# Who makes the lower parts of the expert weights: VectorE alone in place of VectorE and GpSimd

## The chip, the cores and the metric

The kernel runs on one core of a Trainium2 chip. The metric is the device time of one execution in microseconds (us). The kernel before took 1891.57 us, the median of three runs (1889.69 to 1892.58).

## What is computed

One layer of a decoder trunk on 1024 tokens of width 1024. The larger part of it (a modulated norm, one input projection, a recurrent branch, an attention over selected keys, a merge and an output projection) is not touched. The change lies in the mixture of experts that follows: each token goes to 2 of 32 experts, and each expert is a gated network.

```python
def expert_block(args):
    xb, e = args
    hid = jax.nn.silu(xb @ w1[e]) * (xb @ w3[e])   # w1, w3: 1024 x 512
    return hid @ w2[e]                              # w2: 512 x 1024
...
h = h + g2[:, None, :] * hier_moe(u2, ...)
return rmsnorm(h, final_g)
```

All is in float32.

## The kernel before

**Two parts of a number.** TensorE takes each float32 operand as a rounded upper part and a lower part, the rest. ScalarE (ACT) makes the upper part by a copy, and another engine makes the lower part as the difference of the raw number and the upper one. A product of two operands is then three products: upper with upper, upper with lower, lower with upper.

**An expert's weights.** `expert_weights` (L1356 and on) cuts an expert's three matrices into six chunks of 128 x 2048 numbers (1 MB): two of w1, two of w3, two of w2. SP issues each load (`raw_load`, L1377) into a tile of a ring. The ring has 13 tiles at first and shrinks to 7 on the way: `RU` tells how often each of the last places is used. A tile can be loaded again when both engines have read the chunk in it.

`weights` inside `expert` (L1463 to L1475) takes a chunk in two halves of 128 x 1024, g = 0 and 1. For each half it issues the copy `whi` on ACT (L1472) and the subtraction `wlo` (L1474). There are 6 tiles for `whi` and 4 for `wlo` that rotate. Which engine subtracts is decided in one line:

```python
eng = nc.gpsimd if name[0] != "2" and name[-1] == "0" and (g == 1 if e else name[0] == "1") else nc.vector
```

The name is that of the matrix ("1", "3" or "2"), the expert and the chunk. So for every expert but the first, GpSimd (POOL) makes the second half of the first chunk of w1 and of w3, two of the twelve lower parts; for the first expert it makes the two halves of w1's first chunk. VectorE (DVE) makes the rest.

**One expert on the engines.** The rows of an expert's tokens are gathered by POOL's queue (`xg`, L1453), transposed on PE (`ptx`, L1483) and split into `xh` on ACT (L97) and `xl` on DVE (L98). PE sums w1's products in `pa` and w3's in `pb` (L1501), six products of 512 columns for each half chunk, 48 in all. ACT makes `hid` from `pa` (L1506), DVE multiplies it with `pb` (L1507), PE transposes it (`pth`), and it is split into `hh` and `hl`. Then 24 products with w2's parts go to `py` (L137 to L139). DVE scales the sum into `ye` (L1539, two halves), and POOL's queue adds it to the rows in memory by a scatter (`h_spill`, L1543).

Experts overlap. The loop in `experts` steps through the generators of expert e and e - 1 in turn, so that PE does w1 and w3 of one expert, and then w2 of the one before. Within the scheduler's order each engine runs its queue in order: what waits on DVE holds up all that stands behind it there. After the nineteenth expert a branch (`overflow`) takes further blocks of tokens, if an expert has more than 128. `combine` adds the last two experts' parts and makes the final norm.

Of the kernel before, what the change touches and what calls it, by code (L numbers as in the profile page):

```python
# [81 lines left out]
class Trunk:  # L82
# [18 lines left out]
    def as_traced(self, engines):  # L101
        """Each of these engines runs what the block traces in the order in which it is traced."""
# [88 lines left out]
    # ------------------------------------------------------------------  # L191
# [10 lines left out]
    def mod_acc(self, acc, j0, n, ring, last=1):  # L202
        """acc[p, :] = b_mod (row 0) + sum over k of silu(c)[k, p] * w_mod[k, p, :], one k at a time."""
# [15 lines left out]
    def head(self):  # L219
        """Modulated, normalised rows, transposed, and the latent's products, in the order that HEAD gives."""  # L220
        nc, tc, io = self.nc, self.tc, self.io
        x, wm = io["x"][0], io["w_mod"][0][:, : 2 * D].rearrange("p (s c) -> p s c", s=2)
        with ExitStack() as st:
# [53 lines left out]
            def C():  # L277
                """silu(c) as columns"""
                pv = psum("pcol")
                nc.tensor.transpose(pv[:, :KT], cr, self.ident[:KT, :KT])  # L280
                th = hp.tile([P, KT], F32, name="th")
                nc.scalar.activation(th, pv[:, :KT], AF.Tanh, scale=0.5)
                nc.vector.scalar_tensor_tensor(th, th, 1.0, pv[:, :KT], op0=OP.add, op1=OP.mult)
                nc.vector.tensor_scalar(self.csil, th, 0.5, None, op0=OP.mult)

            def Q():
                """The table of square roots comes with this one."""
# [27 lines left out]
            def b(q):  # L315
                """Sums over the partitions; every product's columns are alike, the first of each is left standing."""
# [10 lines left out]
            def e(q):  # L327
                """shift1 and scale1 as columns"""
# [73 lines left out]
    def rsqrt(self, out, m, pool):  # L402
# [5 lines left out]
        # one Newton step: r * (1.5 - 0.5 * m * r * r)  # L408
# [5 lines left out]
    def lru_params(self, lam, hp):  # L414
# [6 lines left out]
        # y = min(|lam|, 80); v = exp(-y) = 2^-n * exp(-f)  # L421
# [15 lines left out]
        # 2^-n from its exponent bits  # L437
# [4 lines left out]
        # log1p(v) = 2 atanh(v / (2 + v))  # L442
# [8 lines left out]
        # softplus(-lam) = max(-lam, 0) + log1p(v)  # L451
# [5 lines left out]
    # ------------------------------------------------------------------  # L457
    def load_in(self, c, m):
        # while the vector engine is taken up by the search, another splits the weights
# [5 lines left out]
    def in_order(self):  # L465
        """Column tiles of w_in in the order of their use, after the latent's."""
# [6 lines left out]
    def next_in(self):  # L473
        """The next column tile; the one after it is already on its way."""
# [6 lines left out]
    def project(self, c0, c1, evac, t0=0):  # L481
        """psum[cols, tokens] of u @ w_in for columns c0..c1, tokens t0.., in column tiles of 128."""
# [15 lines left out]
    def index(self):  # L498
# [4 lines left out]
        with ExitStack() as st:  # L503
            ip = self.pool(st, "idx")
            pp = self.ixp
            # latent
# [24 lines left out]
            # indexer keys: [hi; hi] and [lo; 0]  # L531
# [59 lines left out]
    # ------------------------------------------------------------------  # L591
    def search(self, st):
        """Exact top-256 of each row of scores -> additive bias (s - q) on the selected keys."""
# [33 lines left out]
        # rows whose 256th largest is negative are searched with the sign turned  # L627
        nc.vector.tensor_scalar(t0, cnt, float(TOPK), None, op0=OP.is_ge)
        nc.vector.tensor_scalar(sg, t0, 2.0, -1.0, op0=OP.mult, op1=OP.add)
        for i, j in enumerate(J):  # L630
            n = (j + 1) * P
            # R = 256 where the sign stays, n - 255 where it is turned
# [6 lines left out]
        # On ACT, the count of y >= T is at least R where sum(sign(y - T)) > 2 R - 1 - n, but for T equal to the  # L639
        # R-th value itself, where either may come out: the search ends on it or on the float before it.  # L640
# [22 lines left out]
        # where R or more lie above, the next float is the one  # L663
# [29 lines left out]
    # ------------------------------------------------------------------  # L693
    def gates_q(self, spans):
        """Merge gates and queries, kept in DRAM until their turn."""
# [24 lines left out]
    # ------------------------------------------------------------------  # L720
    def rnn(self):
        nc, io = self.nc, self.io
        with ExitStack() as st:
# [34 lines left out]
            def block(b, xc, xh, xl, gh, gl):  # L758
# [9 lines left out]
                # t = tanh(-log_a / 2), w0 = exp(log_a)  # L768
# [4 lines left out]
                # w = 1 / (1 + t) = (1 + a) / 2, from a = exp(log_a) by one Newton step  # L773
# [3 lines left out]
                # ti = 2 w sqrt(t) * (i x): w1 = -w  # L777
                nc.vector.scalar_tensor_tensor(sq, sq, -2.0, w1, op0=OP.mult, op1=OP.mult)
                nc.vector.tensor_tensor(ti, ti, sq, op=OP.mult)
                # a = 1 - 2 t w  # L780
# [20 lines left out]
    # ------------------------------------------------------------------  # L801
    def attention(self):
# [3 lines left out]
        with ExitStack() as st:  # L806
# [8 lines left out]
            def prep(h):  # L815
                """Keys, queries and, for two heads at a time, values."""
# [131 lines left out]
    # ------------------------------------------------------------------  # L948
    def merge(self, keep, ph):
        """mixT = sigmoid(mgA) * y_aT + sigmoid(mgB) * y_bT."""  # L950
# [26 lines left out]
        # the last places of ring_a hold the merged branches first, 256 tokens in each  # L977
# [16 lines left out]
    def out_w(self, pool, ks):  # L994
        """w_out times gate1, a row block of 128 at a time."""
# [3 lines left out]
        # by halves of the columns, the first half where memory is needed soonest  # L999
# [10 lines left out]
    def branch_load(self, st, br, src, nk, side, g, places):  # L1010
        nc = self.nc
        gp = self.pool(st, f"yg{br}", side=side)
        # in the order of their places, so that the first to be loaded lie where memory is free first
# [10 lines left out]
    def branch_w(self, w, br, nk, c):  # L1024
        """Parts of a column tile, by row blocks; those beyond the eighth in tiles of their own."""
# [45 lines left out]
    def mod_rows(self, st):  # L1071
        """g1, shift2, norm2_g * (1 + scale2), g2 as rows on every partition."""
# [28 lines left out]
    def route_weights(self, st):  # L1101
        """[group | unused | expert] router columns times norm2_g * (1 + scale2), and shift2 through them plus
        the bias, on every partition."""
# [31 lines left out]
    # ------------------------------------------------------------------  # L1135
    def project_out(self):
        """h = x + g1 * (mix @ w_out); u2 rows to DRAM; the routing of each token."""
# [575 lines left out]
```

## Time and profile before

| | |
|---|---|
| median of the runs | 1891.57 us |
| profiled execution (its own time is told by the span alone) | 1894.4 us |
| PE busy | 1778.8 us, 94% |
| DVE busy | 1470.3 us, 78% |
| ACT busy | 1173.6 us, 62% |
| POOL busy | 458.5 us, 24% |
| mean granted clock of TensorE | 0.982 of 2.4 GHz |
| moved by DMA | 366.85 MB |

The profile has one execution's instructions on each engine with start and length, the loads' landings and the semaphores. A group of rows puts alike instructions together: line, engine, operation, output and inputs, shape, count, then the busy time with the mean, then the idle time of the engine just before them with what ended it. A row of stretches gives each engine's busy time (and instructions) in a stretch, the granted clock, the busy share of the 16 DMA engines and what they moved. A product's record is longer than the distance to the next one, since products are pipelined, and a DVE record reaches about 0.07 us into the next one; distances from start to start are what counts.

### The profile page before, as it was taken

Reading aid. Unit: us, or ns where it says so; the run is one execution under the profiler, and the core shown is the slowest. Engines: PE = TensorE matmul, PEld = TensorE weight load, DVE = VectorE, ACT = ScalarE, POOL = GpSimd, SP = SyncE. Lnnn points to the kernel's source line nnn. Section 1 sums busy time; section 2 is a strip of 40 time slices with the busy share of each in tenths; the row PEclk is TensorE's granted clock in tenths of the full one; section 3 lists DMA queues with packets and bytes.
Section 4 is the critical chain, followed back from the end, with each engine's and each line's share of the span. In section 5 each row is a group of like instructions: output and inputs, shape, how many; then the busy total and the mean of one; then the engine's idle time right before and its main releaser. Section 6 shows DMA issues by size and latency. Waiting matters only on the chain.

```text
span 1894.4 us, 24650 instructions
## 1 busy us (share of the span) xinstructions
PE 1778.8 (94%) x8532; PEld 1458.3 (77%) x8532; DVE 1470.3 (78%) x2331; ACT 1173.6 (62%) x1730; POOL 458.5 (24%) x311
## 2 busy tenths in 40 slices
PE   3999999998999999999999989979999999999995
PEld 2788887776777889999788868858778787778774
DVE  6689877696776758777433366479999999999988
ACT  6565677726667758888321023258777777777665
POOL 4101012210010001222000010045454545454444
PEclk9999999998999999999999999979999999999998
DMA  9213754322211222111748444569989999999984
GB/s 295 57 34 111 241 176 150 103 72 65 72 48 61 67 82 75 56 59 60 237 139 265 139 162 178 190 232 354 332 317 333 372 361 364 352 371 359 341 307 157
DMA packets 163738, 366.85 MB, mean 194 GB/s; under 512 B 17855, under 2 KB 107543, under 8 KB 139160
## 3 DMA queue, kind: packets, MB, share of 16 engines
q1 hardware_dynamic: 152112, 340.50, 50.6%
q0 software_dynamic: 10192, 19.99, 4.2%
q10 hardware_dynamic: 1304, 4.74, 0.6%
q8 instruction: 68, 1.11, 0.3%
q14 instruction: 62, 0.51, 0.1%
HBM read 326.90 MB, written 54.53 MB: 201 GB/s over the span
## 4 chain that ended last, share of the span: by engine, by line
PE 56%; DVE 22%; ACT 9%; issue 8%; DMA 3%; POOL 2%; SPq 0%; DVEq 0%; ACTq 0%; POOLq 0%
PE pb L1501 8%; PE pa L1501 6%; DVE wlo L1474 5%; PE py L138 5%; PE py L137 5%; PE py L139 5%; PE pj L139 3%; PE pj L137 3%; PE pj L138 3%; ACT junk_a L654 2%; DVE xc L745 2%; DVE xl L98 1%; PE pout L138 1%; PE pout L137 1%; PE pout L139 1%
## 5 line engine op out<-in xcount | busy, mean ns | idle before, releaser
L1474 DVE TENSOR_TENSOR wlo<-raw_w,whi 128x1024 fp32r<-128x1024 f32 x320 | 479.2, 1542 | 10.2 <-PE pa L1501 3.8
L1472 ACT ACTIVATE whi<-raw_w 128x1024 fp32r<-128x1024 f32 x384 | 398.2, 1059 | 103.5 <-PE pa L1501 29.2
L139 PE MATMUL pj<-uhi,wlo_in 128*128 128x512 f32 (+2 forms) x784 | 303.6, 388 | 5.6 <-POOL wlo_in L128 4.4
L137 PE MATMUL pj<-uhi,whi_in 128*128 128x512 f32 (+2 forms) x784 | 305.1, 389 | 1.2 <-ACT gq L706 1.2
L138 PE MATMUL pj<-ulo,whi_in 128*128 128x512 f32 (+2 forms) x784 | 302.9, 386 | 0.0
L1474 POOL TENSOR_TENSOR wlo<-raw_w,whi 128x1024 fp32r<-128x1024 f32 x64 | 180.9, 2829 | 89.1 <-ACT whi L1472 42.5
L139 PEld LDWEIGHTS pj<-uhi,wlo_in 128*128 128x128 f32 (+1 forms) x784 | 147.0, 187 | 37.5 <-POOL wlo_in L128 6.3
L137 PEld LDWEIGHTS pj<-uhi,whi_in 128*128 128x128 f32 (+1 forms) x784 | 147.3, 188 | 32.3 <-ACT gq L706 2.3
L138 PEld LDWEIGHTS pj<-ulo,whi_in 128*128 128x128 f32 (+1 forms) x784 | 147.1, 188 | 30.2 <-issue 1.0
L654 ACT ACTIVATE junk_a<-B,nt 128x768 bf16<-128x768 f32 (+2 forms) x93 | 96.8, 1041 | 48.9 <-DVE nt L650 40.6
L128 POOL TENSOR_TENSOR wlo_in<-raw_in,whi_in 128x1024 fp32r<-128x1024 f32 (+1 forms) x20 | 51.0, 2550 | 232.8 <-ACT whi_in L127 232.8
L1501 PE MATMUL pa<-whi,xh 128*128 128x512 f32 x256 | 104.5, 408 | 0.6 <-ACT xh L97 0.5
L138 PE MATMUL py<-wlo,hh 128*128 128x512 f32 x256 | 100.8, 394 | 1.3 <-DVE wlo L1474 1.3
L1501 PE MATMUL pa<-whi,xl 128*128 128x512 f32 x256 | 101.6, 397 | 0.1
L137 PE MATMUL py<-gh,whi_y 128*128 128x512 f32 x256 | 99.8, 395 | 1.5 <-ACT gh L97 1.5
L139 PE MATMUL py<-gh,wlo_y 128*128 128x512 f32 x256 | 100.4, 393 | 0.0
L138 PE MATMUL py<-gl,whi_y 128*128 128x512 f32 x256 | 100.3, 394 | 0.1
L1501 PE MATMUL pb<-whi,xh 128*128 128x512 f32 x256 | 100.2, 391 | 0.0
L139 PE MATMUL py<-whi,hl 128*128 128x512 f32 x256 | 100.1, 391 | 0.0
L1501 PE MATMUL pb<-whi,xl 128*128 128x512 f32 x256 | 99.8, 390 | 0.0
L137 PE MATMUL py<-whi,hh 128*128 128x512 f32 x256 | 99.7, 400 | 0.0
L1501 PE MATMUL pb<-wlo,xh 128*128 128x512 f32 x256 | 82.7, 404 | 14.3 <-DVE wlo L1474 7.1
(403 smaller groups left out, 4123.7 us busy)
## 6 DMA issues: line engine op xcount, KB each, us to landing
raw_w<-in_moe_w_dram SPq DMA_DIRECT2D x191, 1024.0 KB, 8.3
raw_in<-in_w_in_dram SPq DMA_DIRECT2D x50, 512.0 KB, 3.5
wm<-in_w_mod_dram SPq DMA_DIRECT2D x32, 512.0 KB, 4.9
sg_spill<-gq SPq DMA_DIRECT2D x16, 512.0 KB, 2.6
sg<-sg_spill SPq DMA_DIRECT2D x32, 256.0 KB, 3.2
wm<-in_w_mod_dram SPq DMA_DIRECT2D x24, 256.0 KB, 5.9
g_spill<-ge SPq DMA_DIRECT2D x10, 512.0 KB, 2.6
gr<-g_spill SPq DMA_DIRECT2D x10, 512.0 KB, 4.8
```

Of the source, the lines that this page charges most:

```text
L98: self.nc.vector.tensor_tensor(lo, src, hi.bitcast(F32), op=OP.subtract)
L128: eng.tensor_tensor(lo[:, :n], raw[:, :n], hi[:, :n].bitcast(F32), op=OP.subtract)
L137: mm(ps, ah, bh, start=start, stop=False)
L138: mm(ps, ah, bl, start=False, stop=False)
L139: mm(ps, al, bh, start=False, stop=stop)
L654: nc.scalar.activation(junk_a[:, :n], self.B[j], AF.Sign, bias=nt[:, i : i + 1], accum_out=cnt[:, i : i + 1])
L745: nc.vector.scalar_tensor_tensor(xc, xr[:, w : w + S], self.cw[:, w * NB + b : w * NB + b + 1], xc, op0=OP.mult, op1=OP.add,)
L1472: self.last_hi = nc.scalar.activation(hi, part, AF.Copy).ins
L1474: eng.tensor_tensor(lo, part, hi.bitcast(F32), op=OP.subtract)
L1501: nc.tensor.matmul(ps, a[:, kk, :], b[:, k * DE : (k + 1) * DE], start=kk == 0 and a is xh and b is hi, stop=kk == KT - 1 and b is lo,)
```

## The change

From the second expert on, the lower parts that POOL made are made on DVE. The first expert's two stay on POOL. The expert of the overflow branch has them on DVE too.

```diff
-                eng = nc.gpsimd if name[0] != "2" and name[-1] == "0" and (g == 1 if e else name[0] == "1") else nc.vector
+                eng = nc.gpsimd if e == 0 and name[0] == "1" and name[-1] == "0" else nc.vector
```

The rest of the difference takes comments away and leaves the code as it is.

The queue of DVE in the middle, for the eleventh expert, where `wlo_10_01` is the second half of a first chunk (12584 is w1's, 12606 is w3's):

```order
 L1474 TENSOR_TENSOR wlo_10_00_12574<-raw_w_10_0_12571,whi_10_00_12573 128x1024
+L1474 TENSOR_TENSOR wlo_10_01_12584<-raw_w_10_0_12571,whi_10_01_12583 128x1024
 L1474 TENSOR_TENSOR wlo_10_00_12596<-raw_w_10_0_12593,whi_10_00_12595 128x1024
 L1539 SCALAR_TENSOR_TENSOR ye_12563<-py_0_12517,gate_l,modrow_3356 128x512
 L1539 SCALAR_TENSOR_TENSOR ye_12563<-py_1_12518,gate_l,modrow_3356 128x512
+L1474 TENSOR_TENSOR wlo_10_01_12606<-raw_w_10_0_12593,whi_10_01_12605 128x1024
 L1474 TENSOR_TENSOR wlo_10_10_12627<-raw_w_10_1_12624,whi_10_10_12626 128x1024
 L1474 TENSOR_TENSOR wlo_10_11_12637<-raw_w_10_1_12624,whi_10_11_12636 128x1024
```

Two subtractions come in; w3's stands behind the two `ye` of the ninth expert, whose products with w2 come just ahead on PE; on POOL it did not.

The queue of POOL near the end, for the experts that the loop counts 28 and 29:

```order
-L1474 TENSOR_TENSOR wlo_28_01_16130<-raw_w_28_0_16117,whi_28_01_16129 128x1024
 L1543 DMA h_spill<-ye_16109,idx 1024x1024
-L1474 TENSOR_TENSOR wlo_28_01_16152<-raw_w_28_0_16139,whi_28_01_16151 128x1024
-L1474 TENSOR_TENSOR wlo_29_01_16303<-raw_w_29_0_16290,whi_29_01_16302 128x1024
 L1543 DMA h_spill<-ye_16282,idx 1024x1024
-L1474 TENSOR_TENSOR wlo_29_01_16325<-raw_w_29_0_16312,whi_29_01_16324 128x1024
```

The scatters stay; before, one stood between the two subtractions of an expert there.

The queue of DVE at the same place:

```order
 L1474 TENSOR_TENSOR wlo_28_00_16120<-raw_w_28_0_16117,whi_28_00_16119 128x1024
 L1539 SCALAR_TENSOR_TENSOR ye_16109<-py_0_16063,gate_l,modrow_3356 128x512
 L1539 SCALAR_TENSOR_TENSOR ye_16109<-py_1_16064,gate_l,modrow_3356 128x512
+L1474 TENSOR_TENSOR wlo_28_01_16130<-raw_w_28_0_16117,whi_28_01_16129 128x1024
 L1474 TENSOR_TENSOR wlo_28_00_16142<-raw_w_28_0_16139,whi_28_00_16141 128x1024
+L1474 TENSOR_TENSOR wlo_28_01_16152<-raw_w_28_0_16139,whi_28_01_16151 128x1024
 L1474 TENSOR_TENSOR wlo_28_10_16173<-raw_w_28_1_16170,whi_28_10_16172 128x1024
```

Here the `ye` come one place earlier than in the middle, so both moved subtractions stand behind them.

## Rows read from the trace of the kernel before

**Rows 1.** The page's costliest groups: the copies and subtractions of the experts' weights.

```profile
L1474 DVE TENSOR_TENSOR wlo<-raw_w,whi 128x1024 fp32r<-128x1024 f32 x320 | 479.2, 1542 | 10.2 <-PE pa L1501 3.8
L1472 ACT ACTIVATE whi<-raw_w 128x1024 fp32r<-128x1024 f32 x384 | 398.2, 1059 | 103.5 <-PE pa L1501 29.2
...
L1474 POOL TENSOR_TENSOR wlo<-raw_w,whi 128x1024 fp32r<-128x1024 f32 x64 | 180.9, 2829 | 89.1 <-ACT whi L1472 42.5
```

**Rows 2.** Stretches of one expert: PE, PEld, DVE, ACT, POOL busy, clock, DMA, GB/s.

```profile
1305.80:1323.55 17.75, 17.75 (x85) 14.89 (x84) 17.75 (x16) 14.45 (x16) 9.93 (x5) 1.00 1.01 367
1323.55:1342.15 18.60, 18.26 (x85) 14.72 (x84) 18.60 (x17) 14.46 (x16) 9.24 (x4) 1.00 0.99 370
1509.56:1528.15 18.59, 18.28 (x85) 14.72 (x84) 18.59 (x17) 14.45 (x16) 9.26 (x4) 1.00 0.97 363
```

**Rows 3.** Timeline of DVE over one expert: start, length in us, then the instruction.

```profile
1506.76 1.27 DVE L98 TENSOR_TENSOR xl<-ptx,xh 128x512 fp32r<-128x512 f32 x2
1507.96 5.89 DVE L1474 TENSOR_TENSOR wlo<-raw_w,whi 128x1024 fp32r<-128x1024 f32 x2
1513.78 1.40 DVE L1539 SCALAR_TENSOR_TENSOR ye<-py,gate_l,modrow 128x512 f32<-128x512 f32 x2
1515.10 4.62 DVE L1474 TENSOR_TENSOR wlo<-raw_w,whi 128x1024 fp32r<-128x1024 f32 x4
1519.64 0.68 DVE L98 TENSOR_TENSOR hl<-pth,hh 128x512 fp32r<-128x512 f32 x1
1520.24 3.48 DVE L1474 TENSOR_TENSOR wlo<-raw_w,whi 128x1024 fp32r<-128x1024 f32 x3
1523.64 0.68 DVE L1507 TENSOR_TENSOR hid<-pb,hid 128x512 f32<-128x512 f32 x1
1524.24 1.21 DVE L1474 TENSOR_TENSOR wlo<-raw_w,whi 128x1024 fp32r<-128x1024 f32 x1
1525.38 1.27 DVE L98 TENSOR_TENSOR xl<-ptx,xh 128x512 fp32r<-128x512 f32 x2
```

**Rows 4.** Timeline of POOL, the same stretch.

```profile
1507.01 2.42 POOL L1474 TENSOR_TENSOR wlo<-raw_w,whi 128x1024 fp32r<-128x1024 f32 x1 [0.99 <-PE py L139]
1509.72 3.06 POOL L1474 TENSOR_TENSOR wlo<-raw_w,whi 128x1024 fp32r<-128x1024 f32 x1 [0.29 <-ACT whi L1472]
```

**Rows 5.** Waits from 1300 to 1800 us: total us, times, longest.

```profile
ACT whi L1472 <- DMA raw_w<-in_moe_w_dram: 0.6, 1, 0.6
```

**Rows 6.** Stretches of the experts' middle, columns as in rows 2.

```profile
1300.00:1750.00 450.00, 442.10 (x2036) 356.48 (x2035) 448.81 (x389) 348.28 (x388) 224.60 (x98) 1.00 0.96 353
...
1300.00:1365.00 65.00, 64.12 (x297) 51.91 (x295) 64.82 (x56) 50.86 (x57) 36.13 (x15) 1.00 1.00 373
1365.00:1370.00 5.00, 4.90 (x23) 4.14 (x24) 5.00 (x7) 3.67 (x4) 2.31 (x1) 1.00 0.37 95
...
1405.00:1415.00 10.00, 10.00 (x50) 8.38 (x49) 10.00 (x12) 8.15 (x11) 3.62 (x3) 1.00 0.49 134
...
1470.00:1597.00 127.00, 124.75 (x576) 100.43 (x575) 127.00 (x110) 99.01 (x110) 62.80 (x27) 1.00 0.99 364
...
1613.00:1750.00 137.00, 134.32 (x622) 108.39 (x621) 137.00 (x121) 104.79 (x119) 66.96 (x30) 1.00 0.98 360
```

**Rows 7.** Stretches of experts 5 to 27 and 28 to 31, columns as in rows 2.

```profile
1323.55:1752.23 428.68, 420.78 (x1933) 338.60 (x1932) 427.66 (x370) 331.64 (x368) 212.25 (x92) 1.00 0.96 352
1752.23:1832.27 80.04, 74.02 (x342) 59.72 (x341) 74.54 (x66) 53.45 (x65) 32.45 (x13) 1.00 0.95 336
```

**Rows 8.** Waits from 1752 to 1845 us: total us, times, longest.

```profile
PE pb L1501 <- POOL wlo L1474: 7.0, 4, 1.9
```

**Rows 9.** Timeline of POOL in the twenty-ninth expert.

```profile
1772.42 2.36 POOL L1543 DMA_INDIRECT h_spill<-ye,idx  x1 [0.16 <-ACT whi L1472]
1774.28 2.88 POOL L1474 TENSOR_TENSOR wlo<-raw_w,whi 128x1024 fp32r<-128x1024 f32 x1
```

**Rows 10.** The stretch around the first of these waits, columns as in rows 2.

```profile
1765.00:1780.00 15.00, 13.29 (x61) 10.75 (x60) 13.94 (x12) 8.91 (x12) 8.28 (x3) 1.00 1.01 349
```

## The prediction

> **What bounds the kernel now.** I read the page's costliest groups first, because they tell where the changed line stands: the subtraction that makes a lower part is there twice, on DVE 320 times at a mean of 1542 ns and on POOL 64 times at 2829 ns [rows 1]. There are 384 copies of upper parts, which is 32 experts of 12, so the overflow loop does not run and the change can touch these 64 subtractions only. The page's line of PE alone (94% busy) would name TensorE as the bound; the stretches by expert show otherwise.
>
> Next come the stretches from one expert's first product to the next one's [rows 2]. One expert takes 84 TensorE instructions: 48 and 24 products of 512 columns and 12 transposes. The reader is to compare three rows. In the first, DVE still had a lead, and the expert took 17.75 us with PE busy throughout. In the other two DVE is busy for the whole stretch, PE has a few tenths of idle time, and the expert takes 18.60 us. So from the fifth expert on VectorE sets the pace, and TensorE's own work is 0.85 us shorter.
>
> Then the two timelines of one such expert. VectorE's rows [rows 3] give the price of each instruction from start to start: four subtractions in a row take 1519.64 - 1515.10 = 4.54 us, 1.135 each; the two `xl` take 1.20, `hl` 0.60, `hid` 0.60 and the two `ye` 1.32. But two subtractions between 1507.96 and 1513.78 take 5.82 us, 2.91 each. GpSimd's rows [rows 4] show why: its two subtractions lie there, from 1507.01 to 1509.43 and from 1509.72 to 1512.78. VectorE's pair ends 1.07 us after the second one's end (1507.96 + 5.89 = 13.85 against 12.78), which is the length of one undisturbed subtraction: it stood until GpSimd was through. The sum of the period is 1.20 + 5.82 + 1.32 + 4.54 + 0.60 + 3.40 + 0.60 + 1.14 = 18.62 us.
>
> Last, what would bind next. The copies on ACT waited for a weight load for 0.6 us in 500 us [rows 5], so the loads are in time now. But the DMA engines are nearly full [rows 6]: 0.96 of 1300 to 1750 us, with two holes, where the ring of raw tiles loses places.
>
> **The change part by part.** All times are against the profiled execution's span of 1894.4 us, which is 2.8 us (0.15%) above the median of the runs, 1891.57; I take the difference off that median.
>
> *GpSimd loses 62 subtractions.* What remains on its queue are one gather and one scatter per expert, which now wait for nothing but their own data. Nobody waits for them sooner, so this costs and gives nothing by itself. SP's queue of loads is the same row for row; its loads are issued as tiles come free.
>
> *VectorE gains 62 subtractions and loses the standing still.* Per expert, 12 x 1.135 + 1.20 + 0.60 + 0.60 + 1.32 = 17.34 us in place of 18.60. That is below TensorE's 17.75, so TensorE becomes the pace unless the order on VectorE holds it up. I worked that through for one place, the new one: the fourth lower part of an expert now stands behind both `ye`, which wait for the last product with w2 that PE does ahead of this expert's own products. From the end of that product VectorE needs 1.32 and 1.135 us, together 2.5, and a signal on top. TensorE asks for this part after three blocks of six products and four products more: 22 products at 17.75 / 78 = 0.228 us (12 half-width transposes counted as six), 5.0 us. So 2.5 us are to spare, less the signal.
>
> *The middle, experts 5 to 27.* These are 23 experts in 428.68 us, 18.64 each [rows 7]. At 17.75 they take 408.3, a saving of 20.4 us. The cover of this saving is the weight stream, and here I have to choose. If the engines move no more per busy microsecond than now, only their idle time can be given up: 4% of 450 us, 18 us (16 to 20 with the rounding), of which the two holes are 0.63 x 5 + 0.51 x 10 = 8.3 us [rows 6]. The holes get shorter because tiles are given back earlier by just what has been saved until then: at 1405 us that is (1405 - 1323.55) / 18.6 = 4.4 experts x 0.85 = 3.7 us. The lead that loads have now, which the near absence of waits in rows 5 shows, can be used up once. I take 18 us, the DMA row's number, since the bound of TensorE lies only 2.4 us above it.
>
> A rule speaks against this term. The Trainium skill, "DMA: Bandwidth & Descriptors", section "Where 436 GB/s comes from", says that for transfers between HBM and SBUF the HBM side binds, at about 358 GB/s per core. The trace speaks against it as a hard limit: 373 GB/s stand over 65 us, 364 over 127 us [rows 6]. By the rule the stream could not go faster than it does, and the sum would be that of the second rival below.
>
> *The end, experts 28 to 32.* Here four experts take 80.04 us, 20.0 each [rows 7], with PE idle for 7.0 us in front of the products with a lower part from POOL, four times [rows 8]. GpSimd's queue has the scatter ahead of that subtraction: 2.36 us of scatter, then 2.88 us of subtraction [rows 9]. This wait goes. What is late next is the lower part that now follows both `ye` as the second of an expert: from the end of the last product 1.32 + 1.135 = 2.5 us and a signal, against ten products, 2.3 us, so at least 0.2 us four times. The term is 7.0 - 0.8 = 6.2 us, and I take 6 for the signals. The ends are 0 and, if these experts too came down to 17.75, 80.04 - 71.0 = 9.0 us and one more wait of 1.75 in the last expert. I stay near the middle because the row names the wait itself.
>
> *Before and after.* The second to fourth experts already run at TensorE's pace, and the closing norm has none of the moved instructions: nothing. The first expert keeps its parts.
>
> **Sum:** 18 + 6 = 24 us; 1891.57 - 24 = 1867.6, told as **1868 us**.
>
> **The rivals.** *TensorE alone sets the pace.* The loads follow at more bytes per busy microsecond; the saving is 20.4 + 9.0 + 1.75 = 31 us, 1860.5 us. For it: the one stretch at 17.75 us had 367 GB/s [rows 2]. Against: the DMA share was 1.01 there, and that stretch lived on tiles already landed.
>
> *The loads bind.* From 1470 us on, where the ring has its smallest size and the shares are 0.99 and 0.98 [rows 6], nothing is gained in the middle. What is left is the gain up to the second hole, 3.7 us as above, and the end's 6: 9.7 us, 1882 us. For it: shares near 1; against: 360 and 364 GB/s there are less than the 373 of the fuller stretch.
>
> *VectorE's subtractions stay slow: slower than before.* If what stretches them is not GpSimd but something else of that place in the period, twelve of them cost the present mean pitch, (18.60 - 3.72) / 10 = 1.49 us, so 21.6 us per expert, 3.0 more than now; over 23 experts 69 us, about 1960 us. It decides at a pitch of (18.60 - 3.72) / 12 = 1.24 us, from which the change costs time. Against it: the seven undisturbed subtractions in two rows of rows 3 (x4 and x3) come at 1.13 to 1.14 us, and VectorE's pair ends right after GpSimd's. The Trainium skill, "Perfetto Trace Analysis", section "Optimizing Scalar/DVE Operations", says that work may sensibly be moved off a saturated VectorE, even to GpSimd, and adds that this might not help as the two share a port; by its first half undoing the move costs time, and rows 3 and 4 bear out the second.
>
> A smaller form of "slower" is that short waits for loads lower TensorE's clock. PE stood still four times for 7.0 us in all at the end [rows 8], and the granted clock of the stretch with the first of these waits is 1.00, the level of 2.4 GHz [rows 10]; I give it no case of its own.
>
> *No change:* the saving of a few microseconds at the end is offset by late loads.
>
> **How the numbers follow.** Forecast (savings of 14 to 28 us) 0.46; TensorE alone 0.24; loads bind 0.20; no change 0.04; slower 0.06. The first three are all faster by over 0.2% (3.8 us, about what a measurement of this kernel can tell from no change): 0.90. The range of 80% reaches from the first rival to the second: low 1860, high 1883; left out are no change, slower, and the outer edges of the two rivals. The forecast's own range is 1863 to 1877.
>
> **What would show it.** Right: POOL's group of this line falls to 2, DVE's rises to 382 with a mean near 1.21 us (records run 0.07 us into the next start) and no maximum above 1.5; experts of the middle take 17.8 to 18.2 us; the DMA share of 1470 to 1750 us is 1.00; ACT's copies now wait for weight loads, for some microseconds in all; the wait of `pb` for POOL is gone. Wrong in size downward: experts at 18.5 with long waits for loads. Wrong upward: 17.75 to the end and GB/s near 385. Wrong altogether: DVE's subtractions above 1.24 us from start to start, or PE waiting for DVE more than now.

## The result and the profile after

| | before | after |
|---|---|---|
| median of the runs | 1891.71 us (1889.69 to 1892.58, 4 runs) | 1865.10 us (1860.44 to 1867.48, 4 runs) |
| profiled execution: its time, its span | 1894.4 us (span) | 1865.06 us, span 1863.3 us |
| mean granted clock | 0.982 | 0.984 |

The ratio is 0.9859 with a 95% interval of 0.9843 to 0.9875: 26.6 us less, 1.4% faster. The spans differ by more, 31.1 us. Of that, 5.4 us lie ahead of the experts, in stages that the change does not touch (the first product with an expert's weights at 1249.89 us against 1255.25). Three executions of the changed kernel had that product at 1249.9, 1252.7 and 1255.9 us, so this part is scatter from execution to execution. From there on 25.7 us are saved.

The page's costliest groups of the changed kernel, for the lines of [rows 1], and the scatter:

```profile
L1472 ACT ACTIVATE whi<-raw_w 128x1024 fp32r<-128x1024 f32 x384 | 395.6, 1057 | 107.8 <-DMA raw_w<-in_moe_w_dram 28.2
L1474 DVE TENSOR_TENSOR wlo<-raw_w,whi 128x1024 fp32r<-128x1024 f32 x382 | 447.9, 1220 | 13.1 <-ACT whi L1472 4.7
...
L1543 POOL DMA_INDIRECT h_spill<-ye,idx x30 | 179.4, 5980 | 215.0 <-DVE ye L1539 202.2
```

DVE makes 382 lower parts, 62 more than before, and is busy with them for 31.3 us less: the mean fell from 1542 to 1220 ns. The copies on ACT now wait mostly for loads; that was for products before.

The stretches: one expert, experts 5 to 27, experts 28 to 31, and three equal pieces of the middle (PE, PEld, DVE, ACT, POOL busy, clock, DMA share, GB/s):

```profile
1512.00:1529.75 17.75, 17.75 (x86) 14.88 (x85) 17.51 (x19) 14.45 (x16) 8.54 (x2) 1.00 1.01 368
1317.98:1728.57 410.59, 409.69 (x1933) 341.92 (x1932) 400.32 (x414) 324.71 (x365) 187.88 (x46) 1.00 0.98 364
1728.57:1803.19 74.62, 73.22 (x341) 59.76 (x340) 69.54 (x73) 56.69 (x67) 12.56 (x4) 1.00 0.99 358
1300.00:1450.00 150.00, 150.00 (x710) 125.77 (x709) 148.06 (x153) 122.18 (x136) 74.13 (x17) 1.00 0.95 351
1450.00:1600.00 150.00, 149.38 (x706) 124.32 (x705) 143.78 (x149) 118.68 (x134) 65.89 (x18) 1.00 0.99 366
1600.00:1750.00 150.00, 148.40 (x696) 122.90 (x695) 144.57 (x152) 113.94 (x132) 59.85 (x15) 1.00 0.99 376
```

An expert takes 17.75 us in place of 18.60, and PE is busy for all of it; DVE is the one with idle time now. Experts 5 to 27 take 410.59 us against 428.68 [rows 7]: 18.1 us. From the start of the twenty-eighth expert to the end it is 134.7 us against 142.1: 7.4 us. With the 0.2 us of the first four experts that is the 25.7.

DVE over one expert, to be read beside [rows 3]:

```profile
1508.92 1.28 DVE L98 TENSOR_TENSOR xl<-ptx,xh 128x512 fp32r<-128x512 f32 x2
1510.12 3.48 DVE L1474 TENSOR_TENSOR wlo<-raw_w,whi 128x1024 fp32r<-128x1024 f32 x3
1513.53 1.40 DVE L1539 SCALAR_TENSOR_TENSOR ye<-py,gate_l,modrow 128x512 f32<-128x512 f32 x2
1514.85 5.75 DVE L1474 TENSOR_TENSOR wlo<-raw_w,whi 128x1024 fp32r<-128x1024 f32 x5
1520.52 0.68 DVE L98 TENSOR_TENSOR hl<-pth,hh 128x512 fp32r<-128x512 f32 x1
1521.12 3.66 DVE L1474 TENSOR_TENSOR wlo<-raw_w,whi 128x1024 fp32r<-128x1024 f32 x3
1524.94 0.69 DVE L1507 TENSOR_TENSOR hid<-pb,hid 128x512 f32<-128x512 f32 x1 [0.15 <-PE pb L1501]
1525.55 1.21 DVE L1474 TENSOR_TENSOR wlo<-raw_w,whi 128x1024 fp32r<-128x1024 f32 x1
```

Where two subtractions took 5.82 us, three now take 1513.53 - 1510.12 = 3.41 us, and five take 5.67. Every one is at 1.135 us. The waits of the copies, from 1300 to 1800 us, in place of [rows 5]:

```profile
ACT whi L1472 <- DMA raw_w<-in_moe_w_dram: 27.7, 30, 2.6
```

At the end, in place of [rows 8], the waits from 1728 to 1845 us:

```profile
PE py L138 <- DVE wlo L1474: 2.7, 4, 0.9
PE pa L1501 <- DVE wlo L1474: 1.1, 1, 1.1
```

No product waits for POOL any more. Smaller waits for DVE are there, with different causes. For the first two of the four on `py`, ACT at 1742 us:

```profile
1742.76 1.06 ACT L1472 ACTIVATE whi<-raw_w 128x1024 fp32r<-128x1024 f32 x1 [2.56 <-DMA raw_w<-in_moe_w_dram]
```

The copy stood for 2.56 us because of a load, so the lower part came late, and PE stood for 0.76 and then 0.47 us. From start to start this costs more than the idle time tells: the twenty-eighth expert took 19.92 us (1728.57 to 1748.49), 2.2 us over 17.75. The other two lie in the last expert, where DVE is stretched again beside POOL's own work for the closing sum:

```profile
1823.98 3.84 POOL L1537 TENSOR_TENSOR ye<-ye,modrow 128x512 f32<-128x512 f32 x2 [5.19 <-ACT ye L1536]
```

```profile
1825.45 3.45 DVE L1474 TENSOR_TENSOR wlo<-raw_w,whi 128x1024 fp32r<-128x1024 f32 x2 [1.04 <-ACT whi L1472]
```

For the wait on `pa`, PE and DVE at the start of the last expert:

```profile
1805.33 0.74 PE L1501 MATMUL pa<-wlo,xh 128*128 128x512 f32 x2 [1.07 <-DVE wlo L1474]
```

```profile
1802.71 1.43 DVE L1539 SCALAR_TENSOR_TENSOR ye<-py,gate_l,modrow 128x512 f32<-128x512 f32 x2 [0.58 <-PE py L139]
1804.06 2.35 DVE L1474 TENSOR_TENSOR wlo<-raw_w,whi 128x1024 fp32r<-128x1024 f32 x2
```

DVE waited for the last product with w2, made the two `ye`, and only then the lower part that PE wanted: the order that the prediction had worked through. In the expert before, the same place cost PE some 0.3 us from start to start (at 1791.97 us); in the other two no wait stands there.

### The profile page after: what moved, and what is told of

It reads as the page before. It is cut to its first block, busy times and chain, and to the rows that moved or that the text cites. A ratio compares the mean times of both kernels' runs of the same rounds, so it can differ in the third digit from the quotient of the medians.

```text
span 1863.3 us, 24597 instructions
## 1 busy us (share of the span) xinstructions
PE 1759.3 (94%) x8532; PEld 1456.1 (78%) x8532; DVE 1439.9 (77%) x2393; ACT 1170.1 (63%) x1730; POOL 398.8 (21%) x249
## 5 line engine op out<-in xcount | busy, mean ns | idle before, releaser
L1474 DVE TENSOR_TENSOR wlo<-raw_w,whi 128x1024 fp32r<-128x1024 f32 x382 | 447.9, 1220 | 13.1 <-ACT whi L1472 4.7
L1543 POOL DMA_INDIRECT h_spill<-ye,idx x30 | 179.4, 5980 | 215.0 <-DVE ye L1539 202.2
L127 ACT ACTIVATE whi_y<-raw_y 128x1024 fp32r<-128x1024 f32 x16 | 17.0, 1062 | 104.5 <-PE py L138 98.6
```

The lines of the kernel that those rows point to most:

```text
L127: nc.scalar.activation(hi[:, :n], raw[:, :n], AF.Copy)
L1474: eng.tensor_tensor(lo, part, hi.bitcast(F32), op=OP.subtract)
L1543: nc.gpsimd.indirect_dma_start(out=self.hd, out_offset=bass.IndirectOffsetOnAxis(ap=idx, axis=0), in_=ye, in_offset=None, bounds_check=S - ...
```

## Experiments

The theory: a subtraction on GpSimd makes VectorE stand, so the two moved subtractions cost VectorE more than making them itself would; without them TensorE's 17.75 us set the pace, with VectorE (17.34) and the loads right behind. The main rivals: the stretching belonged to the place in the period; or TensorE is the only limit and has nothing behind it; or the loads already bind.

### GpSimd's subtractions put back, with nobody waiting for them

```diff
                 with self.tc.issue_after(self.listed) if early else nullcontext():
                     eng.tensor_tensor(lo, part, hi.bitcast(F32), op=OP.subtract)
+                if e in range(1, NE) and name[0] != "2" and name[-1] == "0" and g == 1:
+                    for s_ in (slice(0, 512), slice(512, 1024)):
+                        nc.gpsimd.tensor_tensor(self.pad[:, :512], part[:, s_], hi.bitcast(F32)[:, s_], op=OP.subtract)
                 yield hi, lo
```

> The changed kernel, with GpSimd repeating the subtraction of each half that it used to have (from the same two tiles, into a scratch tile that nobody reads) from the second expert on; every other queue keeps its order, and nobody waits for the copy. My theory (GpSimd's subtraction keeps VectorE standing for its length): VectorE's twelve subtractions get 2 x 1.78 us longer, the expert takes 17.34 + 3.56 = 20.9 us, and over some 27 experts this adds about 85 us, so 1940 to 1960 us. Rival (what stretched the pair before belongs to its place in the period, or to VectorE's own dependences, not to GpSimd): no change against the changed kernel, 1863 to 1869 us. A third way (both engines slow each other to share alike): 1895 to 1920 us.

Measured: 1959.64 us (1958.9 to 1960.37, 2 runs), ratio 1.0361 [1.0331, 1.0391] to the kernel before, 94 us above the changed kernel. One expert of this kernel, then DVE and POOL in another:

```profile
1455.64:1476.67 21.03, 18.91 (x85) 14.57 (x84) 21.03 (x19) 14.67 (x16) 11.95 (x7) 1.00 0.91 333
```

```profile
1453.42 1.28 DVE L98 TENSOR_TENSOR xl<-ptx,xh 128x512 fp32r<-128x512 f32 x2
1454.62 6.67 DVE L1474 TENSOR_TENSOR wlo<-raw_w,whi 128x1024 fp32r<-128x1024 f32 x3
1461.21 1.40 DVE L1542 SCALAR_TENSOR_TENSOR ye<-py,gate_l,modrow 128x512 f32<-128x512 f32 x2
1462.53 5.75 DVE L1474 TENSOR_TENSOR wlo<-raw_w,whi 128x1024 fp32r<-128x1024 f32 x5
```

```profile
1454.44 5.77 POOL L1477 TENSOR_TENSOR pad_at<-raw_w,whi 128x512 f32<-128x512 f32 x3
```

The period is 21.03 us where 20.9 was expected. The rows show the form of it: beside GpSimd's three pieces, VectorE's three subtractions take 6.59 us from start to start of what follows, 3.41 of their own and 3.2 more, about 1.06 for each piece of GpSimd. The two engines take turns. The five subtractions with no subtraction of GpSimd's beside them are at 1.135 us as ever. In the traces DVE, ACT and POOL (but for the added pieces) run their instructions in the same order as in the changed kernel, so the place in the period is not the cause; GpSimd's subtraction is.

### Writes alone, and one input instead of two

```diff
-                    for s_ in (slice(0, 512), slice(512, 1024)):
-                        nc.gpsimd.tensor_tensor(self.pad[:, :512], part[:, s_], hi.bitcast(F32)[:, s_], op=OP.subtract)
+                    nc.gpsimd.tensor_tensor(self.pad[:, :1], part[:, :1], hi.bitcast(F32)[:, :1], op=OP.subtract)
+                    for _ in range(5):
+                        nc.gpsimd.memset(self.pad[:, :512], 0.0)
```

> As the run with repeated subtractions, but GpSimd fills the scratch tile five times with zeros (about 5 x 0.5 = 2.5 us, writes alone, behind one subtraction of a single column that sets the moment). If only work that GpSimd reads with holds VectorE: as the changed kernel, 1863 to 1870 us, with VectorE's subtractions at 1.14 us from start to start. If any work on GpSimd does: again some 1930 to 1960 us. If fills hold it for a part of their length: between. I expect the middle: writes share less, 1866 to 1900 us.

Measured: 1867.74 us (2 runs), ratio 0.9875 [0.9847, 0.9904], no different from the changed kernel. The page's groups:

```profile
L1474 DVE TENSOR_TENSOR wlo<-raw_w,whi 128x1024 fp32r<-128x1024 f32 x382 | 448.2, 1223 | 12.9 <-PE pa L1505 3.7
L1478 POOL MEMSET pad_at<- 128x512 f32 x310 | 166.9, 538 | 16.3
```

GpSimd was busy with fills for 166.9 us, nearly as long as with its subtractions before (180.9 [rows 1]), and VectorE's mean is 1223 ns, as without them. My guess of a partial cost was wrong: fills cost VectorE's subtractions nothing.

They may cost other instructions something. Ahead of the experts, in the changed kernel, two scalings on DVE with one input tile (`r`, a factor per row) lie beside the first expert's two subtractions on POOL (1229.95 to 1234.59 us) and two fills right behind them (to 1236.37); the second row has the same pair a little later, with POOL idle:

```profile
1229.93 6.48 DVE L1310 TENSOR_SCALAR r<-one_k,val 128x32 f32<-128x32 f32 x2
1240.61 0.38 DVE L1310 TENSOR_SCALAR r<-one_k,val 128x32 f32<-128x32 f32 x2
```

The stretched pair ends with the fills (1236.41), not with the subtractions. This was not tried by itself.

```diff
-                        nc.gpsimd.tensor_tensor(self.pad[:, :512], part[:, s_], hi.bitcast(F32)[:, s_], op=OP.subtract)
+                        nc.gpsimd.tensor_copy(self.pad[:, :512], part[:, s_])
```

(against the run with subtractions)

> As the run with repeated subtractions, but GpSimd copies the raw half into the scratch tile (one input instead of two, two pieces of 512 columns per half, two halves per expert); the other queues keep their order. Theory A (any work of GpSimd that reads from the tiles keeps VectorE standing): VectorE's subtractions beside the copies come later by about the copies' length, experts take 19 us or more, 1895 us or longer. Theory B (it takes two inputs on both engines; one-input reading shares like the writes did): experts at 17.75 us and VectorE's subtractions at 1.14 us from start to start, 1863 to 1870 us. I hold B for likelier, about 6 to 4.

Measured: 1877.34 us (2 runs), ratio 0.9919 [0.9897, 0.9942]: between both theories. DVE and POOL in one expert:

```profile
1511.79 4.47 DVE L1474 TENSOR_TENSOR wlo<-raw_w,whi 128x1024 fp32r<-128x1024 f32 x3
1516.19 0.68 DVE L1510 TENSOR_TENSOR hid<-pb,hid 128x512 f32<-128x512 f32 x1
```

```profile
1512.20 6.28 POOL L1477 COPY pad_at<-raw_w 128x512 f32<-128x512 f32 x4
```

The three subtractions beside the copies take 4.40 us in place of 3.41. So three copies made VectorE stand for 1.0 us, where three pieces of a subtraction made it stand for 3.2. Reading counts. A copy is also shorter by itself: the records here have GpSimd's own waiting in them, and where VectorE did not subtract a copy took 0.62 us (at 1251.51) and a piece of a subtraction 1.29 (in the run with subtractions, at 1454.44). How much of the lower price is the shorter instruction and how much the single input was not told apart. `hid` and `xl` beside the copies were not stretched.

The Trainium skill, "SBUF — State Buffer", section "SBUF: two separate sides", states a rule that bears on these three runs: VectorE and GpSimd share a pair of ports as an exclusive lock, and a VectorE instruction with two inputs from the tiles meets it only against a GpSimd instruction that reads them. The turns, the free fills and the unstretched `hid` and `xl` (whose first input is in PSUM, the memory that TensorE's products go to) agree. It also says that the loser is blocked for the whole instruction. That agrees too, although the price is 1.76 us (next run) and the subtraction's record 2.40: its first half microsecond lies beside `xl`, and VectorE is held for the rest.

### Half of the change

```diff
-                eng = nc.gpsimd if e == 0 and name[0] == "1" and name[-1] == "0" else nc.vector
+                first = name[0] == "1" and name[-1] == "0"
+                eng = nc.gpsimd if first and (g == 1 or e == 0) else nc.vector
```

> Half of the change undone: from the second expert on GpSimd keeps the second half of w1's first chunk, VectorE has w3's. My theory (a subtraction on GpSimd costs VectorE 2.91 us for its neighbour in place of 1.135): per expert VectorE has 11 x 1.135 + 3.72 + 1.78 = 17.98 us, 0.23 above TensorE's 17.75 (just not hidden), so about 23 x 0.23 = 5 us over the changed kernel, and at the end half of the 7 us of waits for GpSimd comes back: 1868 to 1876 us. Rival (GpSimd's help is worth what it takes off VectorE, 1.135 us each, and something else made the gain): 1861 to 1866 us, or no longer than the changed kernel.

Measured: 1875.23 us (1873.0 to 1879.68, 6 runs), ratio 0.9918 [0.9900, 0.9937], 10.7 us above the changed kernel that ran beside it (1864.51). One expert, and the subtraction on POOL with DVE's pair beside it:

```profile
1500.87:1518.84 17.97, 17.97 (x86) 14.81 (x85) 17.97 (x18) 14.45 (x17) 5.75 (x4) 1.00 0.99 371
```

```profile
1498.49 2.40 POOL L1475 TENSOR_TENSOR wlo<-raw_w,whi 128x1024 fp32r<-128x1024 f32 x1 [1.45 <-ACT whi L1473]
```

```profile
1499.00 4.11 DVE L1475 TENSOR_TENSOR wlo<-raw_w,whi 128x1024 fp32r<-128x1024 f32 x2
1503.03 1.40 DVE L1540 SCALAR_TENSOR_TENSOR ye<-py,gate_l,modrow 128x512 f32<-128x512 f32 x2
```

The pair takes 4.03 us, 1.76 more than two undisturbed ones, for one subtraction on GpSimd (1.78 was the price from [rows 3]). The period is 17.97 us where the sum said 17.98. GpSimd takes 1.135 us of work off VectorE and costs it 1.76. The rows show how: GpSimd's subtraction began 0.51 us before VectorE's pair, beside `xl`, and ended at 1500.89; the pair ended at 1503.11, 2.22 us later, about the length of two undisturbed subtractions. So VectorE stood until GpSimd was through, as in [rows 4]. A subtraction of GpSimd's that lay beside `xl`, `hid` or `ye` alone should cost VectorE less; that was not tried.

The other term of this expectation, waits for GpSimd at the end, did not come: no product waits for POOL there, and from the twenty-eighth expert on this kernel takes 133.8 us, the changed kernel beside it 133.4. Experts 5 to 27 take 4.9 us more (416.8 against 411.9) and the first four 2.1. So the two profiled executions account for 7.4 us of the 10.7 between the medians; where the rest lies is not shown.

### The end alone

```diff
-                eng = nc.gpsimd if e == 0 and name[0] == "1" and name[-1] == "0" else nc.vector
+                first = name[0] != "2" and name[-1] == "0"
+                on_pool = (g == 1 if e else name[0] == "1") if e in range(27) else False
+                eng = nc.gpsimd if first and on_pool else nc.vector
```

> The change for the last five experts alone (27 to 31); the others keep GpSimd's two lower parts. My theory (the end gains 6 to 8 us because its products wait for GpSimd behind the scatter; the rest of the 26.6 us is won in the middle by the pace): 1891.7 - 7 = 1884 to 1886 us. Rival (the end gains nothing of its own, the whole gain is the pace): 1890 to 1892 us. Rival (the end gains more, since the middle's lead is what the end uses up): 1876 to 1881 us.

Measured: 1883.13 us (1881.57 to 1884.04, 6 runs), ratio 0.9953 [0.9937, 0.9969]: 7.3 us less by the medians, 5.9 to 11.9 by the interval. The middle and the end of this kernel:

```profile
1320.41:1749.20 428.79, 420.80 (x1934) 338.62 (x1932) 427.67 (x370) 331.68 (x368) 210.01 (x91) 1.00 0.96 352
1749.20:1882.00 132.80, 111.59 (x505) 89.80 (x503) 120.03 (x150) 88.25 (x116) 46.82 (x20) 0.94 0.78 286
```

The middle is that of the kernel before (428.68), and the end takes 132.8 us against 142.1: 9.3 us. The two terms of the prediction are separate, and add up: 7.3 here, and about 18 in the middle. The end gains 9.3 here and 7.4 in the changed kernel, since the loads here were never late for the end; in the changed kernel some were, at a cost of 2.2 us in the twenty-eighth expert, which takes 17.75 us here.

### What binds now

```diff
-                    for b, As in ((hi, (xh, xl)), (lo, (xh,))):
+                    for b, As in ((hi, (xh,)), (lo, (xh,))):
```

> Leaves out the products of the inputs' lower part with the upper weights of w1 and w3 (16 of an expert's 78 blocks of work on TensorE); VectorE, ACT and the loads keep all their work. My theory (TensorE sets the pace at 17.75 us, VectorE at 17.34 and the loads stand right behind): an expert comes down to between 17.3 and 17.7 us, so 3 to 12 us are gained in all, 1853 to 1862 us, VectorE busy throughout or ACT waiting for loads. Rival (TensorE alone is the bound and the rest has room): 62/78 x 17.75 = 14.1 us per expert, about 95 us less, near 1770 us.

Measured: 1872.39 us (1868.93 to 1876.42, 3 runs), ratio 0.9897 [0.9863, 0.9931]. With a fifth of an expert's products gone, the time is 7 us longer than that of the changed kernel. One expert, and DVE over it:

```profile
1419.81:1437.80 17.99, 16.48 (x69) 11.43 (x69) 17.54 (x18) 14.33 (x17) 3.88 (x2) 1.00 1.01 377
```

```profile
1419.88 0.69 DVE L1507 TENSOR_TENSOR hid<-pb,hid 128x512 f32<-128x512 f32 x1 [0.29 <-PE pb L1501]
...
1427.02 1.43 DVE L1539 SCALAR_TENSOR_TENSOR ye<-py,gate_l,modrow 128x512 f32<-128x512 f32 x2 [0.17 <-PE py L139]
...
1437.88 0.69 DVE L1507 TENSOR_TENSOR hid<-pb,hid 128x512 f32<-128x512 f32 x1 [0.30 <-PE pb L1501]
```

The rival is refuted: TensorE is not alone. But my own range missed too. VectorE has 17.34 us of work and stands for `pb` and `py` within its fixed order, 0.29 and 0.17 us and smaller steps, and so comes to 18.0. My 17.34 was a sum of work, without the waits that appear as soon as nothing else is slower. Toward the end it is worse: from 1723 to 1817 us five experts take 18.8 us each, and DVE's wait for `pb` is 0.90 us in one of them. The scheduler also orders this program's queues otherwise, so the 7 us are not a price of anything in the changed kernel.

The run with less work still, so that only the loads are left (on top of the last edit):

```diff
+                if name[0] == "2":
+                    self.last_hi = nc.scalar.activation(hi, part, AF.Copy).ins
+                    yield hi, None
+                    continue
...
-            self.mm3(py[f], hh[:, kk, :], hl[:, kk, :], hi[:, s_], lo[:, s_], kk == 0, kk == 3)
+            for a in (hh, hl):
+                nc.tensor.matmul(
+                    py[f], a[:, kk, :], hi[:, s_], start=kk == 0 and a is hh, stop=kk == 3 and a is hl,
+                )
```

> Leaves out the same 16 products, and the lower parts of w2 with their 8 products; VectorE has 8 subtractions per expert, 12.8 us, TensorE 54/78 x 17.75 = 12.3 us, ACT 12 copies and the rest, about 14.5 us. All loads stay. This measures what the loads allow. If the weight stream binds close to the changed kernel's rate (366 to 376 GB/s): an expert takes 17.2 to 17.7 us and the time is 1850 to 1862 us, nearly that of the run with fewer products alone. If the DMA engines can go markedly faster when asked: down to ACT's 14.5 us per expert, about 85 us less, near 1780 us.

Measured: 1849.61 us (1849.49 to 1849.72, 2 runs), ratio 0.9779 [0.9751, 0.9808]. The middle, and eight experts (21 to 28) after the ring has its last size:

```profile
1328.00:1719.50 391.50, 323.54 (x1272) 209.22 (x1272) 275.18 (x297) 291.70 (x339) 66.30 (x42) 0.98 0.98 366
1595.11:1737.19 142.08, 120.78 (x488) 77.98 (x486) 104.80 (x114) 110.37 (x131) 25.85 (x15) 1.00 1.00 377
```

```profile
ACT whi L1469 <- DMA raw_w<-in_moe_w_dram: 42.2, 32, 2.2
ACT whi L1476 <- DMA raw_w<-in_moe_w_dram: 15.7, 28, 1.6
```

With a third of TensorE's work and a third of VectorE's subtractions gone, only 15 us are won. The first six experts run through the tiles that have landed (some 13 us each), and then the weight stream sets the pace: 391.5 us for 21 experts, 18.6 each, and 142.08 / 8 = 17.76 us in the stretch with a share of 1.00. I had expected 17.2 to 17.7. That last figure is TensorE's 17.75. But the stream has no one rate: from 1470 to 1595 us it moved 355 GB/s here at a share of 0.96, where the changed kernel moved 378 from 1470 to 1549 at 17.75 us an expert. Why it was slower here is open. So the changed kernel runs close to two limits at once, with VectorE 0.4 us under them, and its early lead covers the stretches in which loads fall behind.

### A deeper ring

```diff
-RU = [-1, -1, -1, -1, -1, -1, -1, 6] + [3, 3, 4, 4, 4]
+RU = [-1] * 8 + [3, 3, 4, 4, 4]
```

> The changed kernel itself again, beside the runs of this call: 1861 to 1868 us, ratio to the kernel before 0.985 to 0.987.

> The changed kernel with the ring of raw tiles shrinking to eight places in place of seven, so one more load (2.8 us) is under way in the second half of the experts. My theory (at 17.75 us TensorE takes weights about as fast as they come, 366 to 376 GB/s; the lead is gone from 1535 us on, and the late loads near 1743 and 1803 us cost PE 1 to 3 us): those waits become shorter by up to 2.8 us and the time falls by 0 to 4 us, 1861 to 1865 us. Rival (the rate of the loads binds, not the depth of the queue): within 1 us of the changed kernel. Rival (longer queues delay gathers and scatters): 1 to 5 us slower.

Measured side by side: the changed kernel 1864.51 us (5 runs, ratio 0.9860 [0.9842, 0.9878]), eight places 1865.49 us (5 runs, 0.9859 [0.9841, 0.9877]). The copies' waits from 1300 to 1830 us, of the first and of the second:

```profile
ACT whi L1472 <- DMA raw_w<-in_moe_w_dram: 34.7, 35, 2.5
```

```profile
ACT whi L1472 <- DMA raw_w<-in_moe_w_dram: 14.1, 16, 1.5
```

The waits halved, the time did not fall: in the middle they cost PE next to nothing.

```diff
+RU = [-1] * 8 + [7, 7, 7, 7, 7]
```

> The changed kernel with all 13 places of the ring kept until the branch after the nineteenth expert (before, five of them go after the fourth to eighth expert), and eight from there on. The run that measured the loads gave 358 to 377 GB/s when nothing but loads bound, and the deeper ring took the late waits out of the profile without a measurable gain. If the loads' rate binds: the hole in the loads moves to the branch, the weights landed ahead are the same in sum, and the time is that of the changed kernel within 2 us, 1862 to 1867 us. Rival (the early shrinking wastes DMA time, 8 us of holes): lead lasts to the end, 1858 to 1862 us. Rival (more queued loads delay gathers and scatters): 1868 to 1880 us.

> The changed kernel itself, beside the deeper ring in one call: 1863 to 1867 us.

> The changed kernel with 13 places in the ring until the branch, again, to see whether its 3 us below the changed kernel are its own. Theory (the lead of loads kept until the branch takes the late waits of the last experts away, 5 us in the profile): 2 to 5 us less than the changed kernel in this call, 1859 to 1863 us. Rival (executions scatter by that much before the experts begin): within 1.5 us of the changed kernel.

Measured: 1861.55 us (5 runs, ratio 0.9838 [0.9822, 0.9854]), then 1863.81 us (5 runs, 0.9856 [0.9835, 0.9877]) beside 1865.41 us (4 runs, 0.9859 [0.9839, 0.9878]) for the changed kernel. Experts 5 to 27 and 28 to 31 in the first of them:

```profile
1319.31:1729.33 410.02, 409.10 (x1933) 342.08 (x1932) 401.90 (x415) 332.89 (x368) 190.44 (x46) 1.00 0.98 369
1729.33:1800.34 71.01, 71.01 (x337) 59.55 (x336) 70.05 (x73) 57.09 (x64) 28.09 (x5) 1.00 1.01 376
```

The last experts run at 17.75 us too, and PE does not stand. Over all runs, ten with the deeper ring have a mean of 1862.5 us and thirteen of the changed kernel 1865.4: 2.8 us, with some 2 us of uncertainty either way. That is less than the 0.2% that a measurement can tell, so it is a likely gain and not a shown one. The scheduler also orders the last seven experts otherwise there; ring and order were not tried apart.

## Why the prediction was right

The forecast was 1868 us and 1865.1 came, 2.9 us lower; the ratio's interval allows 23.6 to 29.7 us of saving, and 24 was named.

*VectorE's standing still* was read rightly from two timelines, and the runs show the cause. Put back without anyone waiting for it, GpSimd's work costs 94 us; one of the two subtractions costs 1.76 us where 1.78 was worked out; the period of 17.98 came out at 17.97 and that of 20.9 at 21.03. The Trainium skill's half sentence in "Perfetto Trace Analysis", section "Optimizing Scalar/DVE Operations", that moving work to GpSimd might not help because the two share a port, is borne out here by the turns of 1.06 us. Its other half, that such a move may make sense when VectorE is saturated, is not: for this operation it is a net loss of 0.6 us per subtraction.

*The middle* was put at 18 us and measured 18.1 in the profiled pair (410.59; two more executions had 411.85 and 410.11). That the number came out so exactly is luck, because its reason holds only in part. I took it from idle time of the DMA engines, as if loads could give no more. They gave more: 364 GB/s at a share of 0.98, against 352 at 0.96. The middle became 4% shorter: about 2% of this is the share, 1% more bytes per busy microsecond, and 1% weights that had landed before, as far as the rounded figures tell. PE set 17.75 us in nearly every period, and the 2.3 us that are missing to the bound of 20.4 lie in four periods: three around the overflow branch (18.06, 18.89, 18.05) and one with a late load (18.28). So TensorE set this term, and not the idle share of the DMA engines. The stream was close to binding, as the run with the loads alone shows (17.76 us over eight experts, 18.6 over 21). The rival "loads bind" failed all the same: 366 and 376 GB/s stood over 150 us each. That is above the 358 that the Trainium skill names as the limit ("DMA: Bandwidth & Descriptors", section "Where 436 GB/s comes from"); the same page, under "Measured (HBM→SBUF, 128 partitions, SWDGE, issued from GpSimd)", ties that figure to two cores streaming at once. This kernel has one core, so the second reading is the one that the trace bears out, and the prediction should have weighed it.

*The end* was put at 6 us and measured 7.4; alone, with the loads in time, 9.3. The term was mis-sized in three places. The waits for GpSimd are 7.0 us of idle time, but with them went VectorE's own stretching at the end: alone, four experts come down from 80.04 to 72.5 us and the last one gains 1.8 more, nearly the upper end that the prediction had named and not taken. "At least 0.2 us four times" was 1.1 us in the last expert, some 0.3 in the one before, and nothing in the other two. And late loads took 2.2 us back at 1744 us, a wait that I had named as the next one for the middle and had not priced for the end.

*The list of signs.* POOL's group at 2 and DVE's at 382: so, with a mean of 1.220 us. No subtraction above 1.5 us: two were, of 1.78 and 2.31 us, both in the last expert beside GpSimd's own work for the closing sum, which is the same effect again. Experts of the middle at 17.8 to 18.2 us: 17.85 on average. The DMA share: 0.99. Waits of the copies for loads "some microseconds": 27.7 us, more than I had meant, and harmless, as the ring with eight places showed by halving them without a gain.

TensorE's clock stayed at 1.00 of 2.4 GHz through the middle and the last experts, so the short waits had no second price.

## What to carry to other kernels

Before work is shared between VectorE and GpSimd, compare the length of VectorE's instructions with and without GpSimd beside them in the timeline: where both read two inputs from the tiles, the helper cost 1.76 us to save 1.135, because VectorE stood until the helper's instruction was over. Sum the work of every engine and the loads per period of the loop, and expect the next limit to be the second longest of these sums, plus the waits that its fixed order brings. Here three of them lay within about 0.4 us, and taking a fifth of TensorE's products away gained nothing.

## What was not expected of the hardware

A scatter on POOL's queue became three times as long. In one expert of the changed kernel (before it was 2.36 us [rows 9]):

```profile
1515.21 6.85 POOL L1543 DMA_INDIRECT h_spill<-ye,idx  x1 [5.29 <-DVE ye L1539]
1525.98 1.69 POOL L1453 DMA_INDIRECT xg<-n_spill,idx  x1 [3.92 <-PE ptx L1483]
```

Its end comes 6.85 us after its start, 1.54 us after VectorE's five subtractions in a row are over (1520.52). Yet with one subtraction left on GpSimd, or with both repeated, the scatter took 2.31 us beside the same five; with the fills it took 5.20 us, and with the copies 6.85 again. Over the experts of the middle it was short where GpSimd subtracts and mostly long where it does not. Why stays open; nobody waits for it, so it cost nothing here, and it was not tried by itself. That VectorE's five subtractions held it is likely from the rows of the changed kernel and not shown. The Trainium skill tells of such a hold ("SBUF — State Buffer", section "SBUF: two separate sides", the note on GpSimd's descriptors) for VectorE operations that take both ports, such as copies. It does not name subtractions there; the 6.85 us would fit it, the 2.31 us beside the same five do not.
